# A 16-expert layer on one core: gate and up weights by four neighbouring rows per partition, token rows in that column order, the last four experts' rows finished apart

## The chip, the core and the metric

The kernel runs on one core of a Trainium2 chip. The metric is the device time of one execution in microseconds (us); the median of three runs is given, and one further execution was profiled. TensorE is called PE, VectorE DVE, ScalarE ACT, GpSimd POOL, SyncE SP, as in the profile.

## The reference, cut to what matters

512 tokens of width 1024 (16 learned tokens stand ahead of them) pass through one layer: an input LayerNorm, a two-branch mixer with an output projection, a LayerNorm, a mixture of 16 experts, and a last LayerNorm.

```python
h = layer_norm(concat(meta, x), ln_in_g, ln_in_b)
proj = h @ w_in                                   # (528, 9248)
mixed = (gate0 * ssd(proj) @ w_ssd_out + gate1 * pool(proj)) @ w_out
h = layer_norm(2 ** 0.25 * h + mixed, ln1_g, ln1_b)
# router: softmax over 16 experts; the best of 4 groups of 4; the best 2 in it
for e in range(16):
    a = silu(h @ w_gate[e]) * (h @ w_up[e])       # 1024 x 512 each
    out += comb[:, e:e+1] * (a @ w_down[e])       # 512 x 1024
h = layer_norm(2 ** 0.25 * h + out, ln2_g, ln2_b)
return h[:, 16:]
```

All is float32. Each token uses two experts of one group.

## The kernel before

**Head.** The tokens lie in four tiles `xt[t]` of 128 rows. POOL multiplies them by the gain and adds the bias of the input LayerNorm (L531, L532), and SP stores each tile to `h_dram` (L533), from where it is read back as `vt` some 600 us later. The buffers `xt` are then used again by the chain that makes the step sizes of the SSD branch (L538 to L572, on DVE and ACT).

**Mixer.** Until about 680 us PE multiplies by weights that are split into two parts (`wh`, `wl`), three matmuls for one. The output projection ends in `post` (L970): DVE adds the projection's PSUM tile to the tokens' rows in `vt`, half a row (512 columns) at a time. The router, and `place` (L1086), which brings the first two experts' tokens into column form by matmuls against a selection matrix, follow.

**Experts.** `order` lists the experts: the first of each of the four groups, then the second ones, and so on, so that the last four entries are the fourth experts of the four groups, and any four entries in a row from one such round have no token in common. Up to 96 tokens of an expert are gathered from DRAM by `gather` (L264, POOL), transposed in `xprep` (L1113), multiplied in `gu` (L1101, and `gu_third` for tokens beyond 64) and `down` (L1299), and added to `o_dram` by `add_rows` (L1350, two accumulating scatters on POOL). `fetch` (L1239) loads the weights on SP's queue, two loads of 1 MB for each of gate, up and down, into 22 buffers of 1 MB that are handed out in turn by `slot` (L1234).

PE contracts over 128 rows of a weight at a time. Which 128 rows is free as long as the tokens' columns are taken in the same choice. `rows2` puts two neighbouring rows of gate or up in a partition, in runs of 4 KB, and `cols2` takes the tokens' columns in steps of two:

```python
E.dma_start(r.rearrange("p (q j) c -> p q (j c)", j=2),
            src[r0:r0 + n, :].rearrange("(q p j) c -> p q (j c)", p=128, j=2))
...
c0 = k // 2 * 256 + k % 2
return v[:, c0:c0 + 255:2]
```

The rows after the second LayerNorm's gain and bias go to `o_dram` (L1203 to L1208) ahead of the expert loop: DVE writes four tiles of 128x1024, POOL issues their four stores.

**Tail.** The last two experts stand outside the loop (L1519 to L1615), where `InOrder` (L81) keeps DVE, ACT and POOL in the order of the text. Four tiles of `o_dram` are loaded when the add of the fourth expert from the end has landed (`order[12]`, 0-based: experts 13, 14 and 15 are then missing). The class `Finish` (L1409) makes the last LayerNorm of rows: `stats` and `scales` (DVE), or `sums` (ACT), `root` and `steps`; `scaled` (ACT), `gain` (DVE) and `store` (POOL, an accumulating scatter into the output, which holds the last bias already). Tokens of the last three experts are left out of the tiles' stores by the index `rest` and are gathered and finished apart: those of experts 13 and 14 in two tiles `hb`, those of 15 together with its down-projection `pye`, which is kept in PSUM.

Elsewhere the framework's scheduler, which estimates every instruction's time, orders the instructions of each engine.

Of the kernel before, what the change touches and what calls it, by code (L numbers as in the profile page):

```python
# [92 lines left out]
def hybrid_kernel(ctx, tc, x, meta_tokens, ln_in_g, ln_in_b, w_router, w_in, conv_w, conv_b,  # L93
# [60 lines left out]
    for q in range(4):  # L154
# [17 lines left out]
    C_G, C_B, C_CB, C_PS, C_BG, C_NW, C_DT, C_AL, C_DS, C_G1, C_B1 = (  # L172
        0, 8, 16, 48, 56, 72, 88, 89, 96, 112, 120)
# [51 lines left out]
    def rows2(E, r, src, r0):  # L225

        n = r.shape[1] * 128
        E.dma_start(r.rearrange("p (q j) c -> p q (j c)", j=2),
                    src[r0:r0 + n, :].rearrange("(q p j) c -> p q (j c)", p=128, j=2))

    def cols2(v, k):

        c0 = k // 2 * 256 + k % 2
        return v[:, c0:c0 + 255:2]
# [25 lines left out]

    def lim(v):
        return dict(bounds_check=v.shape[0] - 1, oob_is_err=False)

    def gather(dst, src, ix):  # L264
        n = ix.shape[0]
        return G.indirect_dma_start(out=dst[:n], out_offset=None, in_=src, in_offset=off(ix), **lim(src))


    with ExitStack() as p1:
# [120 lines left out]
        xm = hd.tile([NM, D], F32, name="xm")  # L390
# [19 lines left out]
        rows(ln1_g, C_G1, 8)  # L410
        rows(ln1_b, C_B1, 8)
# [241 lines left out]
        Q.dma_start(wr[:, 0], w_router.rearrange("(k p) e -> p k e", p=128))  # L653
        for t in range(NT):
            Q.dma_start(out[t * 128:(t + 1) * 128, :], bcast_row(ln2_b, D))
        for i, v in enumerate((ln1_g, ln1_b)):
            Q.dma_start(gb1[:, i, :].rearrange("p (q j) -> p q j", j=2),
                        flat(v).rearrange("(q p j) -> p q j", p=128, j=2))
        V.tensor_mul(wrg, wr[:, 0], cols[:, C_G1:C_G1 + 8, None].to_broadcast([128, KT, NE]))
        V.tensor_mul(wr[:, 1], wr[:, 0], cols[:, C_B1:C_B1 + 8, None].to_broadcast([128, KT, NE]))  # L660
# [280 lines left out]
        with tc.high_priority():  # L941
# [3 lines left out]
            rows2(G_, first, wu[order[0]], 512)  # L945
# [15 lines left out]
        for r, src, r0 in ((wg_[1], wg[order[0]], 512), (wg_[0], wg[order[0]], 0), (wu_[0], wu[order[0]], 0)):  # L961
            rows2(Q, r, src, r0)
# [15 lines left out]
        def router(t):  # L978
# [107 lines left out]
        def place(t):  # L1086
# [5 lines left out]
            for k in range(KT):  # L1092
                T.matmul(xps[k // 4][:, k % 4, :CAP], lhsT=cols2(vt[t], k), rhs=R0s[t][:, :CAP],
# [589 lines left out]
```

## Time and profile before

| what | us |
|---|---|
| median of 3 runs (lowest, highest) | 1038.21 (1037.29, 1038.98) |
| the profiled execution, its own time | 1038.58 |
| its span in the trace | 1036.8 |
| PE busy in the span | 946.0 |
| DVE, ACT, POOL busy | 594.0, 350.5, 167.5 |
[...]

The 2 us between span and time lie outside what the trace shows. The profile is read by stages: 0 to 680 us is the head and the mixer, 680 to 740 the post-projection, router and first expert, 740 to 975 the expert loop with all weights streaming, 975 to 1024 the last experts and the last LayerNorm; after that the last stores land and the program ends.

### The profile page before, as it was taken

To read this page: it belongs to the slowest core of one execution; us is meant where nothing else is said; L and a number is where in the kernel's file an instruction comes from. 1 tells how busy PE (TensorE), PEld (TensorE's weight loads), DVE (VectorE), ACT (ScalarE), POOL (GpSimd) and SP (SyncE) were. 2 spreads that over 40 slices of the span, in tenths; PEclk is the share of its full clock that TensorE was granted. 3 is DMA by queue.
4 is the path that set the end of the run, shared out by engine and by line. 5 is a ranking of instruction groups with operands and counts; after the bars stand their busy time and mean duration, and the time that the engine had idled before them with its cause. 6 is when DMAs were issued, how large, how long until landed. Compare 5 with 4: busy or idle time off the path is not lost. (4 is left out here: it accounts for less than half of the span.)

```text
span 1036.8 us, 19979 instructions
## 1 busy us (share of the span) xinstructions
PE 946.0 (91%) x8460; PEld 757.0 (73%) x8460; DVE 594.0 (57%) x1180; ACT 350.5 (34%) x503; POOL 167.5 (16%) x150
## 2 busy tenths in 40 slices
PE   4879999999999999999999897999779788999980
PEld 3878888999899898989898785877545344564550
DVE  6877671376869696978878778666520101001173
ACT  4344332532435252433425353224112121112252
POOL 4930000000000000000000226200212121212343
PEclk9999999999999999999999998999989899999996
DMA  7442446422323142333332423977899999999744
GB/s 220 138 162 100 131 131 178 122 82 82 134 90 128 56 151 74 123 102 123 102 122 72 153 91 133 379 290 304 293 367 372 373 373 374 371 372 373 251 123 78
DMA packets 98739, 199.43 MB, mean 192 GB/s; under 512 B 10272, under 2 KB 56968, under 8 KB 97616
## 3 DMA queue, kind: packets, MB, share of 16 engines
q1 hardware_dynamic: 83392, 163.78, 44.8%
q0 software_dynamic: 9392, 18.61, 7.2%
q10 hardware_dynamic: 5856, 15.61, 4.1%
q8 instruction: 76, 1.25, 0.5%
q14 instruction: 23, 0.19, 0.1%
HBM read 185.79 MB, written 19.79 MB: 198 GB/s over the span
## 5 line engine op out<-in xcount | busy, mean ns | idle before, releaser
L255 DVE TENSOR_TENSOR wl<-raw,wh 128x2048 fp32r<-128x2048 f32 (+1 forms) x49 | 111.7, 2283 | 53.2 <-ACT wh L252 53.0
L252 ACT CAST wh<-raw 128x2048 fp32r<-128x2048 f32 (+1 forms) x49 | 87.9, 1798 | 143.6 <-PE ss L800 64.1
L307 PE MATMUL mm<-hH,wh 128*128 128x264 f32 x624 | 128.7, 287 | 6.1 <-ACT ze L599 5.4
L89 PE MATMUL gu<-raw,xT 128*32 128x256 f32 (+1 forms) x2592 | 126.8, 344 | 7.8 <-issue 4.0
L307 PE MATMUL mm<-hH,wl 128*128 128x264 f32 x624 | 128.0, 286 | 0.0
L307 PE MATMUL mm<-hL,wh 128*128 128x264 f32 x624 | 127.3, 285 | 0.0
L89 PEld LDWEIGHTS gu<-raw,xT 128*32 128x32 f32 x2592 | 82.8, 110 | 48.8 <-issue 16.8
L1153 DVE TENSOR_TENSOR sg<-sg,gu 128x128 f32<-128x128 f32 x13 | 3.7, 288 | 182.5 <-ACT sg L1152 182.5
L307 PEld LDWEIGHTS mm<-hH,wh 128*128 128x128 f32 x624 | 99.1, 190 | 9.4 <-ACT ze L599 5.6
L809 POOL TENSOR_TENSOR acc<-acc,pre 128x512 f32<-128x512 f32 x12 | 19.1, 1614 | 530.5 <-ACT pre L808 530.5
L325 PE MATMUL mm<-hH,wh 128*128 128x512 f32 x256 | 102.5, 401 | 0.0
L325 PE MATMUL mm<-hL,wh 128*128 128x512 f32 x256 | 101.6, 397 | 0.0
L325 PE MATMUL mm<-hH,wl 128*128 128x512 f32 x256 | 101.5, 396 | 0.0
L307 PEld LDWEIGHTS mm<-hH,wl 128*128 128x128 f32 x624 | 98.0, 189 | 1.2 <-DVE wl L255 0.2
L307 PEld LDWEIGHTS mm<-hL,wh 128*128 128x128 f32 x624 | 97.4, 189 | 0.2
L89 PE MATMUL py<-raw,hT 128*32 128x512 f32 (+1 forms) x704 | 73.8, 558 | 5.2 <-issue 4.6
L800 PE MATMUL ss<-wh,yy 128*128 128x512 f32 x192 | 67.3, 410 | 0.0
L89 PEld LDWEIGHTS py<-raw,hT 128*32 128x32 f32 x704 | 23.5, 116 | 46.2 <-issue 39.2
L325 PEld LDWEIGHTS mm<-hH,wl 128*128 128x128 f32 x256 | 48.2, 188 | 10.5
L325 PEld LDWEIGHTS mm<-hH,wh 128*128 128x128 f32 x256 | 48.1, 188 | 10.3
L325 PEld LDWEIGHTS mm<-hL,wh 128*128 128x128 f32 x256 | 48.0, 188 | 10.3
L1256 POOL DMA_INDIRECT o_dram<-ys,ixq x26 | 40.5, 1557 | 74.3 <-ACT ys L1354 70.7
(391 smaller groups left out, 1584.1 us busy)
## 6 DMA issues: line engine op xcount, KB each, us to landing
raw<-in_w_exp_down_dram SPq DMA_DIRECT2D x30, 1024.0 KB
raw<-in_w_in_dram SPq DMA_DIRECT2D x28, 1024.0 KB
raw<-in_w_exp_up_dram SPq DMA_DIRECT2D x28, 1024.0 KB
raw<-in_w_exp_gate_dram SPq DMA_DIRECT2D x26, 1024.0 KB
M<-aD ACTq DMA_DIRECT2D x8, 1024.0 KB
raw<-in_w_in_dram SPq DMA_DIRECT2D x16, 512.0 KB
raw<-in_w_ssd_out_dram SPq DMA_DIRECT2D x8, 1024.0 KB
ze<-eD ACTq DMA_DIRECT2D x16, 256.0 KB
```

The lines of the kernel that those rows point to most:

```text
L89: return lambda *a, **k: self.tc.keep_in_program_order(f(*a, **k))
L252: A.copy(wh[:, c], src[:, c])
L255: (E[i] if E else V).tensor_sub(wl[:, c], src[:, c], wh[:, c])
L307: T.matmul(ps[:, i, :HF], lhsT=w[:, k, cs], rhs=h[k][:, i * HF:(i + 1) * HF], start=(n == 0), stop=(n == 3 * KT - 1))
L325: T.matmul(ps, lhsT=w[:, k, cs], rhs=h[k][:, NM:], start=(n == 0), stop=(n == 3 * KT - 1))
L800: T.matmul(ps, lhsT=y[:, j, t * 128:(t + 1) * 128], rhs=w[:, j, hf * 512:(hf + 1) * 512], start=(n == 0), stop=(n == 5))
L809: G.tensor_add(a, a, f)
L1153: V.tensor_mul(sg[:, 256:384], sg[:, 256:384], p3[:, 128:])
L1256: return G.indirect_dma_start(out=dst, out_offset=off(ix), in_=src[:n], in_offset=None, **lim(dst), **kw)
```

## The change

It has three parts. Gate and up weights go four neighbouring rows to a partition (one run of 8 KB for each partition and load, 512 rows a load), and the tokens' rows from the output projection on are kept in that column order: within each half row of 512, column 4r+j stands at 128j+r. `xprep`, `place` and the router then read neighbouring columns. Rows go into that order where POOL adds the first LayerNorm's bias (`by4`), where `post` reads PSUM, and back (`back4`) where the rows go to `o_dram`; since `xp` is a further buffer, each `h_dram` store leaves from the buffer that the tile before lay in. `o_dram` is written in half rows, by ACT's queue instead of POOL's. In the tail, four experts' rows instead of three stand apart, and the four tiles are loaded and finished one expert earlier; expert 13's rows get scales by themselves.

```diff
-    def rows2(E, r, src, r0):
+    def fours(E, r, src, r0):
+        E.dma_start(r.rearrange("p j c -> p (j c)"), src[r0:r0 + 512, :].rearrange("(p j) c -> p (j c)", j=4))
+    def by4(v):
+        return v.rearrange("p (r j) -> p j r", j=4)
+    def back4(v):
+        return v.rearrange("p (j r) -> p r j", j=4)
...
+        xp = hd.tile([128, D], F32, name="xp", tag="xm", bufs=1)
         for t in range(NT):
             G.tensor_mul(xt[t], xt[t], gb[:, 0, :])
-            G.tensor_add(xt[t], xt[t], gb[:, 1, :])
-            Q.dma_start(h_dram[t * 128:(t + 1) * 128, :], xt[t])
+            for c in (slice(0, 512), slice(512, 1024)):
+                G.tensor_add(xp[:, c].rearrange("p (j r) -> p j r", j=4), by4(xt[t][:, c]), by4(gb[:, 1, c]))
+            Q.dma_start(h_dram[t * 128:(t + 1) * 128, :], xp)
+            xp = xt[t]
...
-            V.scalar_tensor_tensor(vt[t][:, c], vt[t][:, c], ALPHA, pso, op0=OP.mult, op1=OP.add)
+            v = vt[t][:, c].rearrange("p (j r) -> p j r", j=4)
+            V.scalar_tensor_tensor(v, v, ALPHA, by4(pso), op0=OP.mult, op1=OP.add)
...
-                T.matmul(xps[k // 4][:, k % 4, :CAP], lhsT=cols2(vt[t], k), rhs=R0s[t][:, :CAP],
+                T.matmul(xps[k // 4][:, k % 4, :CAP], lhsT=vt[t][:, k * 128:(k + 1) * 128], rhs=R0s[t][:, :CAP],
...
-                    T.transpose(ps[i][:, k, :n], cols2(xg[:n], 4 * i + k), ident[:n, :n])
+                    T.transpose(ps[i][:, k, :n], xg[:n, (4 * i + k) * 128:(4 * i + k + 1) * 128], ident[:n, :n])
...
             for t in range(NT):
-                V_.tensor_mul(vt[t], vt[t], g1B)
-                V_.tensor_add(vt[t], vt[t], b1B)
-                G.dma_start(o_dram[t * 128:(t + 1) * 128, :], vt[t])
+                for c in (slice(0, 512), slice(512, 1024)):
+                    V_.tensor_mul(to.rearrange("p (r j) -> p r j", j=4), back4(vt[t][:, c]),
+                                  g1B[:, c].rearrange("p (r j) -> p r j", j=4))
+                    V_.tensor_add(to, to, b1B[:, c])
+                    A.dma_start(o_dram[t * 128:(t + 1) * 128, c], to)
+                    to = vt[t][:, c]
...
-                for e_ in order[-3:]:
+                for e_ in order[-4:]:
...
+    fin = Finish(fv[:NT] + rows4[:3], None)
+    add_to(down(i - 2, w2), i - 2)
+    rows_of(3, 1)
+    rows_of(0, 0)
+    for t in range(NT):
+        fin.stats(t)
+    fin.scales(slice(0, NT))
     pg = gu(wg2)
...
+    for t in range(NT):
+        fin.scaled(t)
+        fin.gain(t)
+    fin.store(0, rest[:, 0:1])
+    add_to(down(i - 1, w3), i - 1)
+    for t in range(1, NT):
+        fin.store(t, rest[:, t:t + 1])
...
     py = down_split(us, hhl)
-    fin.scaled(NT - 1)
-    fin.gain(NT - 1)
-    for t in range(2, NT):
-        fin.store(t, rest[:, t:t + 1])
-    fin.sums(NT)
-    fin.stats(NT + 1)
+    fin.sums(NT + 1)
+    fin.scales(slice(NT + 1, NT + 2))
+    fin.scaled(NT + 1)
+    fin.stats(NT + 2)
...
+    for n in (3, 2):
+        fin.gain(NT + n)
+        fin.store(NT + n, ix_of(last - 3 + n))
```

How the instructions move, at three places. SP's queue in the head: `raw<-in_w_in_dram` are the mixer's weights, `h_dram<-xt` the four stores. Before:

```order
L298 DMA raw<-in_w_in_dram 128x8x256 x2
L605 DMA raw<-in_w_pool_dram 128x2x256
L533 DMA h_dram<-xt 128x1024
L298 DMA raw<-in_w_in_dram 128x8x256
L533 DMA h_dram<-xt 128x1024 x3
```

Now:

```order
L310 DMA raw<-in_w_in_dram 128x8x256 x2
L618 DMA raw<-in_w_pool_dram 128x2x256
L310 DMA raw<-in_w_in_dram 128x8x256
L545 DMA h_dram<-xp 128x1024
L545 DMA h_dram<-xt 128x1024 x2
L310 DMA raw<-in_w_in_dram 128x8x256
L545 DMA h_dram<-xt 128x1024
```

All four stores stand behind a third weight load, and the last one behind a fourth.

POOL's queue in the tail (`o_dram<-ys` are the adds of an expert's rows, `raw<-o_dram,idx` and `hb<-o_dram,idx` the gathers of rows that stand apart, `out_dram<-raw,rest` the stores of the four tiles). Before, from the add of expert 13:

```order
L89 DMA o_dram<-ys_6570,ixq_113 1024x512
L89 DMA o_dram<-ys_6570,ixq_114 2048x256
L1307 UNCONDITIONAL_BRANCH
L89 DMA hb<-o_dram,idx 96x1024
L89 DMA o_dram<-ys_6569,ixq_113 1024x512
L89 DMA o_dram<-ys_6569,ixq_114 2048x256
L1134 UNCONDITIONAL_BRANCH
L89 DMA hb<-o_dram,idx 96x1024
L89 DMA out_dram<-raw,rest 512x1024 x4
L89 DMA out_dram<-hb,idx 512x1024 x2
L89 DMA out_dram<-raw,idx 512x1024
```

Now, from the store of the first tile:

```order
L89 DMA out_dram<-raw,rest 512x1024
L89 DMA o_dram<-ys_6589,ixq_113 1024x512
L89 DMA o_dram<-ys_6589,ixq_114 2048x256
L89 DMA out_dram<-raw,rest 512x1024 x3
L1327 UNCONDITIONAL_BRANCH
L89 DMA o_dram<-ys_6588,ixq_113 1024x512
L89 DMA o_dram<-ys_6588,ixq_114 2048x256
L89 DMA hb<-o_dram,idx 96x1024
L1148 UNCONDITIONAL_BRANCH
L89 DMA out_dram<-hb,idx 512x1024
L89 DMA raw<-o_dram,idx 96x1024
L89 DMA out_dram<-hb,idx 512x1024
```

The tiles' stores moved ahead of the last add (expert 14's); behind it stand four stores of single experts' rows, two more following the last line shown.

DVE's queue at the very end, from the last part of the split of expert 15's hidden rows (`raw<-pt,raw`). Before:

```order
L89 TENSOR_TENSOR raw<-pt,raw 128x4x32
L89 TENSOR_TENSOR raw<-raw 128x1024
L89 BN_STATS st<-hb 128x6 x2
L89 BN_AGGR mvf<-st 128x2
L89 SCALAR_TENSOR_TENSOR raw<-pye,wsl,raw 96x512
L89 BN_STATS st<-raw 128x6
L89 TENSOR_SCALAR rsf<-mvf 128x2
```

Now:

```order
L89 TENSOR_TENSOR raw<-pt,raw 128x4x32
L89 TENSOR_SCALAR rsf<-mvf 128x1
L89 TENSOR_SCALAR rsf<-rsf 128x1 x7
L89 SCALAR_TENSOR_TENSOR rsf<-mvf,rsf 128x1
L89 BN_STATS st<-raw 128x6 x2
L89 BN_AGGR mvf<-st 128x2
L89 SCALAR_TENSOR_TENSOR raw<-pye,wsl,raw 96x512
L89 BN_STATS st<-raw 128x6
L89 TENSOR_TENSOR hb<-hb,raw 128x1024
L89 SCALAR_TENSOR_TENSOR raw<-pye,wsl,raw 96x512
```

The fourth tile's gain is gone from here; the nine small instructions of expert 13's scales and the gain of its rows stand in the row now.

## Rows read from the trace of the kernel before

**Rows 1.** Windows: busy us (x count) of PE, PEld, DVE, ACT, POOL, clock, DMA share, GB/s.
```profile
733.00:975.00 242.00, 212.26 (x3400) 122.69 (x3396) 38.81 (x123) 47.15 (x122) 57.89 (x47) 0.94 1.02 370
```
**Rows 2.** Waits of PE, 733 to 975 us: total us, times, longest.
```profile
PE pt L89 <- DMA xg<-h_dram,idx: 9.3, 1, 9.3
```
**Rows 3.** DMA queues, 733 to 975 us: packets, MB, share of 16 engines.
```profile
q1 hardware_dynamic: 20720, 79.86, 86.3%
q0 software_dynamic: 5600, 8.95, 14.8%
...
raw<-in_w_exp_up_dram SPq DMA_DIRECT2D x22, 1024.0 KB
```
**Rows 4.** DMA, 888 to 892 us: only weight packets of 4 KB move.
```profile
DMA packets 423, 1.63 MB, mean 408 GB/s; under 512 B 25, under 2 KB 25, under 8 KB 423
```
**Rows 5.** DMA, 315.54 to 317.14 and 370.96 to 372.56 us: only 8 KB packets move.
```profile
DMA packets 84, 0.69 MB, mean 430 GB/s; under 512 B 0, under 2 KB 0, under 8 KB 0
DMA packets 81, 0.66 MB, mean 415 GB/s; under 512 B 0, under 2 KB 0, under 8 KB 0
```
**Rows 6.** Timeline and groups of PE's weight loads: every second column; neighbouring; `place`.
```profile
968.82 1.04 PEld L89 LDWEIGHTS pt<-ident,xg 96*128 96x128 f32 x8 [0.27 <-issue]
977.51 0.31 PEld L89 LDWEIGHTS pt<-ident,sg 128*128 128x128 f32 x3 [0.41 <-issue]
L89 PEld LDWEIGHTS pso<-xg,v 128*128 128x128 f32 x64 | 7.8, 196 | 1.2 <-ACT to L1067 0.6 <-DVE xg L1053 0.6
```
**Rows 7.** Groups of DVE: `post`; a reduction that reads apart; a product of neighbours.
```profile
L972 DVE SCALAR_TENSOR_TENSOR v<-v,pso 128x512 f32<-128x512 f32 x7 | 4.7, 676 | 4.9 <-PE pso L89 4.9
L663 DVE TENSOR_REDUCE raw<-wrg 128x16 f32<-128x128 f32 x1 | 0.4, 371 | 0.0
L659 DVE TENSOR_TENSOR wrg<-raw,cols 128x128 f32<-128x128 f32 x1 | 0.3, 293 | 1.8 <-DMA raw<-in_w_router_dram 1.8
```
**Rows 8.** Groups of POOL: the head's adds, the `o_dram` stores.
```profile
L532 POOL TENSOR_TENSOR xt<-xt,gb 128x1024 f32<-128x1024 f32 x4 | 12.9, 3258 | 0.0
L1208 POOL DMA_DIRECT2D o_dram<-v x4 | 2.2, 554 | 8.4 <-DVE v L89 8.4
```
**Rows 9.** Timeline, 60 to 72 us: start, us, engine, line, operation, idle before.
```profile
60.36 2.10 SPq L533 DMA_DIRECT2D h_dram<-xt  x3
67.75 0.43 DVE L543 TENSOR_SCALAR xt<-xt 128x528 f32<-128x528 f32 x1 [2.96 <-DMA h_dram<-xt]
70.98 0.81 PE L307 MATMUL mm<-hH,wh 128*128 128x264 f32 x2 [5.40 <-ACT ze L599]
```
**Rows 10.** Timeline of the tail, 981 to 1025 us.
```profile
981.28 2.41 SPq L1530 DMA_DIRECT2D raw<-o_dram  x4
981.79 0.62 DVE L89 TENSOR_TENSOR sg<-sg,gu 128x256 f32<-128x256 f32 x2 [10.49 <-PEq L1134]
987.90 1.64 PEld L89 LDWEIGHTS gu<-hb,xT 128*32 128x32 f32 x32
1007.32 5.80 PE L89 MATMUL pye<-raw 128*96 128x512 f32 x24 [1.60 <-ACT raw L89]
1008.69 1.23 ACT L89 ACTIVATE raw<-raw,rsf 128x1024 f32<-128x1024 f32 x1
1009.83 1.04 ACT L89 ACTIVATE raw<-hb 128x1024 f32<-128x1024 f32 x1
1011.10 1.28 DVE L89 BATCH_NORM_STATS2 st<-hb 128x6 f32<-128x512 f32 x2
1019.91 1.23 DVE L89 TENSOR_TENSOR raw<-raw 128x1024 f32<-128x1024 f32 x1 [0.22 <-ACTq L1623]
1019.97 2.48 POOL L89 DMA_INDIRECT out_dram<-hb,idx  x1 [0.59 <-DVE hb L89]
1022.75 1.43 POOL L89 DMA_INDIRECT out_dram<-raw,idx  x1 [0.30 <-issue]
```
**Rows 11.** DMA, 1012 to 1016 us: the accumulating stores' queue.
```profile
q0 software_dynamic: 259, 0.61, 101.3%
```

More of the change, by code (lines that the diff above doesn't have):

```diff
@@ L258, in off, with queued @@
         return bass.IndirectOffsetOnAxis(ap=ix, axis=0)
+    queue = []
+    def queued(f):
+        if not queue:
+            return f()
+        with tc.issue_after(queue[-1]):
+            r = f()
+        queue.append(r.ins)
+        return r
     def lim(v):
@@ L944, in hybrid_kernel @@
                 G_.dma_start(vt[t], h_dram[t * 128:(t + 1) * 128, :])
-            rows2(G_, first, wu[order[0]], 512)
+            fours(G_, first, wu[order[0]], 512)
             G_.dma_start(g1B, bcast_row(ln1_g, D))
@@ L1530, in hybrid_kernel, with rows_of, add_to @@
         last_['SP'] = Q.dma_start(fv[t], o_dram[t * 128:(t + 1) * 128, :]).ins
-    rows3 = fv[NT:NT + 3]
-    for v in rows3:
+    rows4 = fv[NT:]
+    for v in rows4:
         G.memset(v, 0.0)
-    gather(XG[(i + 1) % 2], h1_dram[:, :], ix_of(i + 1))
+    queue.append(gather(XG[last % 2], h1_dram[:, :], ix_of(last)).ins)
+    i = last - 1
+    V, A, G = (InOrder(tc, e_) for e_ in (V, A, G))
+    def rows_of(k, n):
+        ins = gather(rows4[k], o_dram[:, :], ix_of(last - 3 + k)).ins
+        if n:
+            apart(ins, n)
+        gets.append(ins)
+    def add_to(p, k):
+        for sc in add_rows(p, k):
+            for g_ in gets:
+                tc.declare_no_dep(sc, g_, reason="experts of different groups have no token in common")
+    gets = []
+    fin = Finish(fv[:NT] + rows4[:3], None)
[5 more added lines that the diff above has]
+    fin.scales(slice(0, NT))
     pg = gu(wg2)
@@ L1548, in hybrid_kernel, with part @@
     on = spare[1]
-    V.memset(fl(on)[CAP:], 0.0)
-    for w, (wh, wl) in zip(wd_, us):
-        A.copy(wh, w)
-        V.tensor_sub(wl, w, wh)
-    add_rows(down(i - 1, w3), i - 1)
-    def rows_of(k, ins, n):
-        ins.append(gather(rows3[k], o_dram[:, :], ix_of(last - 2 + k)).ins)
-        return ins[-1]
-    gets = []
-    apart(rows_of(2, gets, 2), 2)
-    rows_of(0, gets, 0)
-    fin = Finish(fv[:NT] + rows3[:2] + [fl(on)], fl(spare[0]))
-    tiles = slice(0, NT)
-    for t in range(NT):
-        fin.stats(t)
-    fin.scales(tiles)
+    fin.rows.append(fl(on))
+    fin.junk = fl(spare[0])
+    for t in range(NT):
[5 more added lines that the diff above has]
+        fin.store(t, rest[:, t:t + 1])
+    V.memset(fl(on)[CAP:], 0.0)
+    def part(k):
+        A.copy(us[k][0], wd_[k])
+        V.tensor_sub(us[k][1], wd_[k], us[k][0])
+    part(0)
+    fin.stats(NT)
+    fin.scales(slice(NT, NT + 1))
     pg = gu(wg_)
@@ L1571, in hybrid_kernel @@
     sg = silu(pg)
-    for sc in add_rows(down(i, wp_), i):
-        for g_ in gets:
-            tc.declare_no_dep(sc, g_, reason="experts of different groups have no token in common")
-    for t in range(NT - 1):
-        fin.scaled(t)
-        fin.gain(t)
-    for t in range(2):
-        fin.store(t, rest[:, t:t + 1])
-    rows_of(1, gets, 0)
+    part(1)
+    add_to(down(i, wp_), i)
+    rows_of(1, 1)
+    fin.scaled(NT)
+    fin.gain(NT)
+    fin.store(NT, ix_of(last - 3))
+    rows_of(2, 0)
     act(None, gu(wu_), p3=gu_third(last, (wg_, wu_)), sg=sg)
```

76 lines of the change are left out of this document (32 added, 44 removed).

## The prediction

> **What bounds the kernel now.** I read the busy times by stage first, because the change touches three stages with different limits. Until 733 us PE is the bound and the change does not alter its work there. From 733 to 975 us the DMA engines are: their share is 1.02, while PE is idle for 242 - 212.26 = 29.7 us [rows 1]. The reader is to see the two columns together, the full DMA share beside a PE that waits. The largest of these waits, 9.3 us for the third expert's gathered rows [rows 2], stands at the start of the stretch and costs nothing, since the weights arrive no faster for it; the other 20.4 us are shared out over the experts, mostly as waits for weights. The queues' view says what fills the DMA: 79.86 of 89.42 MB are weights on queue q1 [rows 3]. In the last two experts PE is the bound again, up to the last matmul, 1007.32 + 5.80 = 1013.1 us [rows 10]. Behind that stands a chain on DVE, ACT and POOL to the end of the last issue, 22.75 + 1.43 = 1024.2 us [rows 10], and the accumulating stores fill their queue for a part of it [rows 11]. Then the last store lands and the program ends, 12.6 us later; I leave this piece as it is.
>
> So a gain must come from the rate of the weights, from PE's last two experts or from the closing chain, and a loss from the head's order or from that chain.
>
> **The change, part by part.** The profiled execution took 1038.58 us, 0.37 above the median of the runs; sums go against the former, and the forecast is brought to the median at the end.
>
> *A. Runs of 8 KB.* The trace has both sizes. Where 4 KB weight packets move alone, the rate is 408 GB/s [rows 4], so a load of 1.049 MB takes 2.57 us. Where 8 KB packets move alone, it is 430 and 415 GB/s [rows 5], on average 422, and a load would take 2.49 us. By queue the same: 86.3% of 242 us on 16 engines over 20,720 packets is 161 ns for one of 4 KB [rows 3], so 256 of them take 2.58 us on 16 engines. 48 gate and up loads are issued from 733 us on, 24 of each (22 of the 24 up loads are the row in [rows 3]). 48 x 0.085 = **-4.1 us**. It counts in full, since it is taken from the stretch that the DMA bounds, and what PE has left to wait (20.4 us) is more than that. Bounds: nothing, if the mixed traffic has another limit; 48 x (2.57 - 2.44) = -6.3 at the better of the two rates. [...]
>
> *B. Neighbouring columns for PE.* In `xprep` 8 weight loads that read every second column take 1.04 us, 0.130 each; 3 that read neighbours take 0.31, 0.103 each [rows 6]. That is 0.2 us for an expert, of which the two experts that PE bounds count (0.4), and 16 x 0.027 = 0.4 for the last tile's `place`, whose loads are of the slow kind (196 ns) [rows 6]. I take **-0.7**; bounds -0.8 and 0.
>
> *C. `post` reads PSUM 16 bytes apart.* Now 676 ns for 512 columns [rows 7]. The nearest row that reads apart is a reduction over 128 columns, 371 ns, against 293 for a product of neighbours [rows 7]: at most 0.08 x 4 = 0.3 us. Seven of the eight lie beside PE's work, and only the last is waited for. **+0.2**, bounds 0 and +0.4.
>
> *D. `o_dram` in half rows on ACT's queue.* The four stores on POOL wait 8.4 us for DVE [rows 8], with the third expert's gather behind them; that gather now goes first and PE's 9.3 us wait becomes shorter, but the weights cover it. 1024 packets of 2 KB replace 512 of 4 KB in the stretch that the DMA bounds. A line through 161 ns at 4 KB and 311 ns at 8 KB (2.49 us x 16 / 128) gives 86 ns at 2 KB: (1024 x 86 - 512 x 161) / 16 = +0.35 us. ACT's eight issues wait for DVE, and behind them stand `xT` and `hT` of the first experts, where the DMA covers a delay. **+0.3**, bounds 0 and +1.
>
> *E. Head.* Four adds of 3258 ns on POOL [rows 8] become eight of half the size whose reads are 16 bytes apart; no row shows POOL reading so, and DVE's row bounds it at 371/293, 1.27 times, +3.4 us for the four. Then the stores: they are issued at 60.36 us, DVE waits 2.96 us for one of them to free its buffer, and PE waits 5.40 us soon after, for ACT [rows 9]. Each buffer is now freed by a later store, and the last store stands behind one more weight load that waits for its own buffer. What follows on DVE is the step-size chain and the next split of weights, which has about 5 us in hand. I take **+0.7**; bounds -0.5 (the issue order brings a weight load forward) and +5.
>
> *F. Tail.* The four tiles are loaded one expert earlier, so the issue at 981.28 us [rows 10] comes forward; their statistics stand on DVE ahead of expert 14's work, and DVE was idle for 10.49 us there [rows 10]. If the loads land about 5 us after the last weights, and 3.7 us of statistics and scales and 1.9 of `sg` and `xT` follow, PE's next need at 987.90 [rows 10] still has 2 us in hand. At the end: ACT no longer scales the fourth tile (1.23 us), so the sums of expert 13's rows begin at 1008.7 instead of 1009.83 [rows 10] and, at 2.64 us for the three large and small steps, end at 1011.3. Then DVE's new row: nine small instructions (2.2 us, as the nine of the four tiles' scales took), statistics of expert 14 (1.28 + 0.2), to 1015.0 where they began at 1011.10 before [rows 10]; first half product and its statistics 1.4, gain 1.2, second half 1.6 (by the 0.68 of `post` [rows 7] for a product, as much for its statistics), `root` and `steps` 1.3, to 1020.5; a scaling of 1.24 and then two gains, the second behind the second scaling, to 1024.2 where the last gain ended at 1019.91 + 1.23 = 1021.1 [rows 10]. The last issue would end at 1025.9 instead of 1024.2, since POOL's slow issue of 2.48 us [rows 10] loses its cause when the four tiles' stores have gone ahead. **+1.8**; bounds -2.5 (chain covered, that second of POOL and a shorter queue at the end) and +3.
>
> Sum: -4.1 - 0.7 + 0.2 + 0.3 + 0.7 + 1.8 = **-1.8 us**, 1036.8 for the profiled execution and **1036.4** for the median.
>
> **The rivals.** *1. The end is set by the stores' queue, not by the chain.* The queue of accumulating stores is full from 1012 to 1016 us [rows 11], and 2 MB of the four tiles pass it ahead of the last rows. Moved forward by a whole expert, they free it, and the last landing follows its issue at once. With F = -0.7 (what the queue gives back, 2.5, against the 1.8) and E = 0 the sum is -4.3: 1033.9. For it: the full queue and the slow issue of 2.48 us. Against it: the queue has gaps from 1018 us on, before the last issue.
>
> *2. The head stalls, and the kernel is slower.* POOL's strided adds and the last `h_dram` store behind a waiting weight load keep a buffer of the step-size chain; DVE, in order, sits before it, and the split of the next weights (2.3 us) comes late for PE. It decides once the store is more than about 5 us later. At twice that, PE loses about 6 in place of 0.7: +3.5, 1041.7. For it: DVE waited for such a store already [rows 9]. Against it: the 1.27 times from DVE's row give only 3.4 us. [...]
>
> *3. The longer runs bring nothing.* The two 8 KB stretches last 1.6 us each and carry nothing else, while the loop mixes weights with gathers and adds (q0: 14.8% of the time for a tenth of the bytes [rows 3]). If that mixture sets the rate, A is 0 and the sum is +2.3: 1040.5. For it: the mean over the whole stretch is 370 GB/s [rows 1], well below either rate. Against it: the weights' packets alone account for 86.3%.
>
> **How the numbers follow.** A difference under 0.2%, 2.1 us, can't be told from none. My forecast has a chance of 0.45 with a range of 1034.5 to 1038.5; its centre lies near the border, so 0.19 of it is faster and 0.26 the same. Rival 1 has 0.23, all faster. Rival 2 has 0.16, slower. Rival 3 has 0.10, of which 0.06 slower and 0.04 the same. 0.06 is left for parts that cancel, the same. Faster 0.42, same 0.36, slower 0.22. The range goes from 1031.3 (A at its better rate in rival 1, -2.2, and some of B's and C's play) to 1042.5 (rival 2 and D's bound).
>
> **What would show it.** In the changed profile: 733 to 975 us shorter by about 4 us, with 128 packets a gate or up load and about 311 ns a packet (A); weight loads of `xprep` near 0.10 us each (B); `post` under 1 us (C); PE's wait for the third expert's rows gone with no effect on the end (D); PE's first large wait still near 5 us and no new one of more than 2 us before 100 us (E); from the last matmul's end to the end of the last issue 13 us instead of 11 (F). I am wrong if the loop's stretch keeps its length, if PE shows a new wait in the head, or if statistics of the tiles hold `xT` of the last expert.

## The result and the profile after

The changed kernel is slower, where the forecast was 1036.4 us and its range ended at 1042.5.

| what | before | after |
|---|---|---|
| median, us (runs) | 1038.60 (4) | 1052.86 (4) |
| lowest, highest | 1037.29, 1040.06 | 1049.70, 1055.52 |
| ratio, with its 95% interval | | 1.0136 [1.0116, 1.0156] |
| the profiled execution, its own time | 1038.58 | 1049.70 |
| its span | 1036.8 | 1048.0 |
| its mean granted TensorE clock, share of full speed | 0.969 | 0.965 |

The profiled execution after is the fastest of its four, so the trace shows 11.1 of the 14.3 us. To place them I cut both spans at three instructions: SP's issue of the loop's first `down` load (731.17 us before, 732.14 after), the start of the loop's last transposes on PE, of the rows of expert 14 counted from 0 (968.82 [rows 6], now 971.00), and the end of the last issue (1024.18 [rows 10], now 1034.16 + 1.42 = 1035.58).

| stretch | before | after | difference | forecast |
|---|---|---|---|---|
| head and mixer | 731.17 | 732.14 | +1.0 | +0.7 (E) |
| expert loop | 237.65 | 238.86 | +1.2 | -4.3 (A to D) |
| tail, to the last issue | 55.36 | 64.58 | +9.2 | +1.8 (F) |
| to the end of the span | 12.62 | 12.42 | -0.2 | 0 |

**The loop.** The first row is the windows view of 733 to 975 us (columns as in [rows 1]), the second PE's largest wait there, the third SP's wait for a store, the fourth the weights' queue in the same stretch, the fifth the DMA view of 840 to 844 us, where weights move almost alone; the last two are from the kernel before, 733 to 975 us: SP's wait for a store, and the only waits of PE for weight loads in its list.

```profile
733.00:975.00 242.00, 208.33 (x3415) 118.04 (x3405) 42.38 (x131) 46.00 (x120) 56.58 (x43) 0.94 1.01 370
...
PE pt L89 <- DMA xg<-h_dram,idx: 9.8, 1, 9.8
...
SPq L1266 <- DMA o_dram<-v: 12.5, 3, 9.2
...
q1 hardware_dynamic: 14625, 80.07, 85.6%
...
DMA packets 246, 1.66 MB, mean 414 GB/s; under 512 B 40, under 2 KB 40, under 8 KB 48
...
SPq L1246 <- DMA o_dram<-v: 5.8, 2, 5.2
...
PE gu L89 <- DMA raw<-in_w_exp_down_dram: 1.0, 3, 0.3
```

The mean rate is 370 GB/s as before, at the same clock (0.94) [rows 1]: nearly a third of the packets are gone, and the bytes move no faster. PE's wait for the third expert's rows was to become shorter and is 9.8 us instead of 9.3 [rows 2]. SP waits for a store of `o_dram`, up to 9.2 us at once (5.2 before). Almost alone, 8 KB packets run at 414 GB/s, where 4 KB ones had 408 [rows 4].

Why the gather is not earlier stands on POOL's timeline (start, us, engine, line, operation, idle before it and what ended that):

```profile
747.96 0.95 POOL L1273 MEMSET xg<- 128x1024 f32 x1 [11.19 <-DMA o_dram<-room]
749.18 1.65 POOL L278 DMA_INDIRECT xg<-h_dram,idx  x1 [0.27 <-POOL xg L1273]
```

The stores left POOL's queue, as meant. But the first half row goes through a scratch buffer `room`, and the buffer of the third expert's rows is laid over it: POOL's memset waits 11.19 us for that store to land, and the gather is issued 17.04 us after the loop's first `down` load, where it was 16.77.

**Small loads, `post`, head.** PE's weight loads of `xprep` (the first row is that of the loop's last transposes) and `place` (the second row, a group); DVE's `post`; POOL's adds in the head and the last store of `h_dram`:

```profile
971.00 0.70 PEld L89 LDWEIGHTS pt<-ident,xg 96*128 96x128 f32 x8 [2.44 <-issue]
...
L89 PEld LDWEIGHTS pso<-xg,v 128*128 128x128 f32 x64 | 7.5, 192 | 1.2 <-ACT to L1081 0.6 <-DVE xg L1067 0.6
...
L986 DVE SCALAR_TENSOR_TENSOR v<-v,pso x7: 632/686/689, 682.5 to 710.1; 128x512 f32<-128x512 f32 x7
...
49.15 5.17 POOL L544 TENSOR_TENSOR xp<-xt,gb 128x512 f32<-128x512 f32 x2
54.28 18.55 POOL L544 TENSOR_TENSOR xt<-xt,gb 128x512 f32<-128x512 f32 x6
72.86 0.32 SPq L545 DMA_DIRECT2D h_dram<-xt  x1
```

Eight loads of neighbouring columns take 0.70 us (1.04 before [rows 6]); `place` has 192 ns for 196. `post` has a median of 686 ns before and after: here the reads of PSUM 16 bytes apart cost nothing. POOL's adds take 5.17 + 18.55 = 23.72 us instead of 12.9 [rows 8], 1.84 times, and the last `h_dram` store is issued at 72.86 us, where all four were out by 62.46 [rows 9]. That the adds are now halves is not the reason: POOL's twelve adds of 128x512 neighbouring columns later in the mixer (`acc<-acc,pre`) take 1620 ns on average, half of 3258.

**The tail.** First the DMA view (KB each, median us from issue to landing) of 945 to 970 us, then that of 970 to 991 us; then the timeline, whose last row is from the kernel before:

```profile
o_dram<-ys,ixq POOLq DMA_INDIRECT x3, 9.3
...
raw<-o_dram SPq DMA_DIRECT2D x4, 512.0 KB, 11.6
...
o_dram<-ys,ixq POOLq DMA_INDIRECT x2, 3.7
```

```profile
971.37 2.68 SPq L1551 DMA_DIRECT2D raw<-o_dram  x4
981.50 1.29 DVE L89 BATCH_NORM_STATS2 st<-raw 128x6 f32<-128x512 f32 x2 [8.35 <-DMA raw<-o_dram]
986.16 1.55 POOL L89 DMA_INDIRECT o_dram<-ys,ixq  x1 [15.80 <-ACT xT L89]
989.68 4.64 ACT L89 ACTIVATE raw<-raw,rsf 128x1024 f32<-128x1024 f32 x4 [3.97 <-DVE rsf L89]
996.94 0.47 ACT L89 COPY hT<-pt 128x384 f32<-128x384 f32 x1
997.47 5.34 PE L89 MATMUL py<-raw,hT 128*32 128x512 f32 x32 [3.69 <-ACT hT L89]
1009.28 1.54 POOL L89 DMA_INDIRECT o_dram<-ys,ixq  x1 [0.31 <-issue]
1012.77 5.79 PE L89 MATMUL pye<-raw 128*96 128x512 f32 x24 [1.60 <-ACT raw L89]
1017.05 1.06 ACT L89 ACTIVATE raw<-hb 128x1024 f32<-128x1024 f32 x1 [2.82 <-DMA hb<-o_dram,idx]
1030.20 2.36 DVE L89 TENSOR_TENSOR raw<-raw 128x1024 f32<-128x1024 f32 x2 [1.36 <-ACT raw L89]
1031.70 2.15 POOL L89 DMA_INDIRECT out_dram<-raw,idx  x1 [4.08 <-DVE raw L89]
1034.16 1.42 POOL L89 DMA_INDIRECT out_dram<-raw,idx  x1 [0.30 <-issue]
...
991.50 1.56 POOL L89 DMA_INDIRECT o_dram<-ys,ixq  x1 [12.29 <-DMA raw<-o_dram]
```

The four tiles are loaded one expert earlier, but that expert is still among the weights: the adds issued there take 9.3 us to land, and 3.7 later. So the loads are issued at 971.37, only 9.9 us before the old 981.28 [rows 10], and land 11.6 us after that (median of the four). Two queues then wait for them, and in both `InOrder` keeps the order of the text:

- ACT scales the tiles only when DVE has their scales, at 989.68. Behind the four scalings stand the copy `hT` of expert 14's hidden rows (996.94) and with it PE, which waits 3.69 us for it (0.62 before). The 32 matmuls behind that wait then take 5.34 us, where e5 below has 3.64 for the same ones: the granted clock from 990 to 1000 us is 0.89 (1.00 before). PE's last matmuls begin at 1012.77, 280.6 us after the loop's first `down` load (276.15 before).
- POOL's next add into `o_dram`, expert 12's rows, may not overwrite what is still being read, and goes at 986.16 (974.50 for its like before). The row names ACT as what ended 15.80 us of idleness, but `ys` had been done since 976.6; what ended it is the loads' landing, as the like row of e2 below names it. In the kernel before the first add behind the loads waited for them too, to 991.50, 10.2 us after their issue. Behind the add stand the tiles' stores, which wait for the scalings and gains: expert 14's add goes at 1009.28, the gather of expert 13's rows at 1012.98, their sums at 1017.05 where I had 1008.7.

From the last matmul's end to the end of the last issue it is 1035.58 - 1018.56 = 17.0 us, against 11.1 before and 13 in the forecast.

### The profile page after: what moved, and what is told of

The parts are those of the page before. It is cut to its first block, busy times and chain, and to the rows that moved or that the text cites. A ratio compares the mean times of both kernels' runs of the same rounds, so it can differ in the third digit from the quotient of the medians.

```text
span 1048.0 us, 20025 instructions
## 1 busy us (share of the span) xinstructions
PE 944.6 (90%) x8460; PEld 752.7 (72%) x8460; DVE 608.0 (58%) x1208; ACT 352.3 (34%) x504; POOL 184.5 (18%) x153
## 5 line engine op out<-in xcount | busy, mean ns | idle before, releaser
L822 POOL TENSOR_TENSOR acc<-acc,pre 128x512 f32<-128x512 f32 x12 | 19.2, 1620 | 521.0 <-ACT pre L821 521.0
L89 PE MATMUL py<-raw,hT 128*32 128x512 f32 (+1 forms) x704 | 75.9, 567 | 10.4 <-issue 6.7
L1276 POOL DMA_INDIRECT o_dram<-ys,ixq x24 | 37.3, 1553 | 69.2 <-ACT ys L1374 65.6
```

What stands on the lines that cost most here:

```text
L89: return lambda *a, **k: self.tc.keep_in_program_order(f(*a, **k))
L822: G.tensor_add(a, a, f)
L1276: return queued(lambda: G.indirect_dma_start(out=dst, out_offset=off(ix), in_=src[:n], in_offset=None, **lim(dst), **kw))
```

## The experiments

Ratios are against the kernel before, with 95% intervals.

### Which part: the two halves apart

*e1*: the change with the tail of before. *e2*: the kernel before with the tail of the change.

```diff
-                for e_ in order[-4:]:
+                for e_ in order[-3:]:
...
-    queue.append(gather(XG[last % 2], h1_dram[:, :], ix_of(last)).ins)
+    gather(XG[(i + 1) % 2], h1_dram[:, :], ix_of(i + 1))
```

> The changed kernel with the closing part of the kernel before (last three experts' rows apart, tiles loaded behind expert 12's add); runs of 8 KB and the new column order stay. Theory 1, the new tail lost the time: 1039 to 1042 us, and the last matmul ends within 3 us of the kernel before. Theory 2, the head and the expert loop lost it and the tail only inherits: 1048 us or more.

> The kernel before with the new closing part alone (last four experts' rows apart); weights in runs of 4 KB and the old column order. Theory 1: 1047 to 1051 us, with the add of expert 12 waiting about 10 us for the tiles' loads. Theory 2: within 3 us of the kernel before.

Measured: e1 1.0051 [1.0027, 1.0074], e2 1.0143 [1.0116, 1.0171]. Both halves lose. e1 should have won 3.6 us by terms A to E and loses 5; in its profile none of that lies in the loop (237.4 us against 237.65), 4.3 us lie ahead of the loop's first `down` load and 2.4 in the tail. The tail alone loses 14.9 where F had 1.8. In e2 the chain is that of the change: the add of expert 12 waits for the loads, and PE for `hT`.

```profile
985.78 1.55 POOL L89 DMA_INDIRECT o_dram<-ys,ixq  x1 [17.46 <-DMA raw<-o_dram]
...
997.28 6.60 PE L89 MATMUL py<-raw,hT 128*32 128x512 f32 x32 [4.53 <-ACT hT L89]
```

The two do not add up: 0.51 + 1.43 is more than the 1.36 per cent of both together. What the two halves share, or which of the runs' scatter makes up the rest, I did not find.

### The tail: what stands behind the waits

*e5*: the change, with the tiles' scaling, gain and stores moved behind expert 14's add and both gathers. *e5b*: the same in e2.

```diff
-    for t in range(NT):
-        fin.scaled(t)
-        fin.gain(t)
-    fin.store(0, rest[:, 0:1])
     add_to(down(i - 1, w3), i - 1)
-    for t in range(1, NT):
-        fin.store(t, rest[:, t:t + 1])
...
     rows_of(1, 1)
+    rows_of(2, 0)
+    for t in range(NT):
+        fin.scaled(t)
+        fin.gain(t)
+        fin.store(t, rest[:, t:t + 1])
     fin.scaled(NT)
     fin.gain(NT)
     fin.store(NT, ix_of(last - 3))
-    rows_of(2, 0)
```

> The changed kernel, with the four tiles' scaling, gain and stores moved behind the add of expert 14 and behind both gathers of the rows of 13 and 14, on ACT, DVE and POOL; the tiles' loads and statistics stay as early as in the change. If the loss of the tail is the place of this work in ACT's and POOL's order (PE waits 3.7 us for hT behind it; expert 13's rows are gathered at 1013 us behind the tiles' stores): PE's wait goes, the last matmul ends about 3 us earlier, the sums of expert 13's rows begin at least 4 us earlier, and the time falls by 4 to 8 us. If the loss is that add 12 waits for the tiles' loads: add 12 still starts near 986 us and the time stays within 2 us of the changed kernel.

> The same order of the tail as e5_late_tiles, on the kernel before with 4 KB runs (e2_new_tail with that one edit). By the first theory 4 to 8 us under e2_new_tail; a time under the kernel before would make four experts' rows apart worth having without the rest of the change.

Measured: e5 1.0105 [1.0068, 1.0142] against the change's 1.0136, e5b 1.0065 [1.0046, 1.0084] against e2's 1.0143. Between e5 and the change the intervals overlap; between e5b and e2 they do not. The trace of e5:

```profile
988.05 1.55 POOL L89 DMA_INDIRECT o_dram<-ys,ixq  x1 [16.25 <-ACT xT L89]
...
997.25 3.64 PE L89 MATMUL py<-raw,hT 128*32 128x512 f32 x32 [0.62 <-ACT hT L89]
...
1012.65 7.93 PE L89 MATMUL pye<-raw 128*96 128x512 f32 x24 [1.60 <-ACT raw L89]
...
1014.02 1.04 ACT L89 ACTIVATE raw<-hb 128x1024 f32<-128x1024 f32 x1
```

PE's wait for `hT` is back at 0.62 us, as before the change, and its last matmuls begin at 277.7 instead of 280.6 (both from the loop's first `down` load). The sums of expert 13's rows begin 1.4 us after that (4.3 in the change), although the add of expert 12 waits as long as in the change (16.25 us): what made them late is the tiles' work ahead of them, not that wait. From the end of the last matmul to the end of the last issue it is 12.0 us, and 13 was forecast, but that meets by luck: the last matmuls take 7.93 us here (5.79 in the change), and the granted clock from 1000 to 1024 us is 0.86 (0.93 in the change). From their start it is 19.9 us, where the forecast comes to 18.6. In e5b PE has other waits in their place:

```profile
993.69 3.07 PE L89 MATMUL gu<-raw,xT 128*32 128x256 f32 x32 [2.82 <-DVE xT L89]
```

Here it is the tiles' statistics on DVE that hold the last expert's columns, one of the three signs by which the prediction said that it would be wrong; in the change and in e5 PE does not wait there.

*e6*: the change, with the tiles' loads issued by POOL, so that SP's queue can't be what delays them.

```diff
...
-        last_['SP'] = Q.dma_start(fv[t], o_dram[t * 128:(t + 1) * 128, :]).ins
+        G.dma_start(fv[t], o_dram[t * 128:(t + 1) * 128, :])
```

> The changed kernel with the four tiles' loads issued by POOL instead of SP, so that they don't stand behind 14 us of weights on SP's queue. If that queue makes add 12 wait: it starts at 978 to 981 us instead of 986.2, and the time falls by 3 to 6 us. If the transfers as such are too slow beside the weights, add 12 starts within 2 us of 986 and the time stays.

Measured: 1.0136 [1.0095, 1.0177], the change's own ratio.

```profile
974.77 2.26 POOL L1551 DMA_DIRECT2D raw<-o_dram  x4 [1.27 <-DMA o_dram<-ys,ixq]
...
990.08 1.65 POOL L89 DMA_INDIRECT o_dram<-ys,ixq  x1 [13.05 <-ACT xT L89]
```

The loads still wait for expert 11's add to land, and expert 12's add goes as late behind them (254.1 us after the loop's first `down` load, 254.0 in the change); SP's queue is not the cause.

### The loop: length of the runs

*e3*: the kernel before with one run of 8 KB a partition. *e7*: with runs of 2 KB. Both leave out the matching order of the tokens' columns (as does e9 below): they do the same work on other pairs of numbers. The diff is e3's.

```diff
-        E.dma_start(r.rearrange("p (q j) c -> p q (j c)", j=2),
-                    src[r0:r0 + n, :].rearrange("(q p j) c -> p q (j c)", p=128, j=2))
+        E.dma_start(r.rearrange("p j c -> p (j c)"), src[r0:r0 + 512, :].rearrange("(p j) c -> p (j c)", j=4))
```

> The kernel before, with gate and up loads in runs of 8 KB and nothing else; the tokens' columns stay as they were, so the experts' matmuls pair other columns with other rows. If a load of 8 KB runs is faster by the 0.085 us that I forecast: 1034 to 1035 us. If by a third of that: about 1037. If not at all: 1038 to 1039, and the loop's stretch keeps its mean rate of 370 GB/s.

> The kernel before with gate and up loads in runs of 2 KB (one row for each partition and part); the tokens' columns stay as they were, so the experts' matmuls pair other columns with other rows. Theory: a small transfer waits behind the packets of the weights' queue, the longer they are the longer (the third expert's gather lands 9.0 us after its issue at 4 KB, 11.9 at 8 KB). Then at 2 KB it lands in less than 8 us and SP's longest wait for the o_dram stores is under 5.2 us, and the time is 1034 to 1039 us, as far as the shorter packets' own cost allows. Rival: the longer runs stream worse by themselves; then the latency of the gather is 9 us as before and the time within 2 us of the kernel before.

Measured: e3 1.0048 [1.0032, 1.0065], e7 1.0035 [1.0017, 1.0053]. 8 KB runs alone lose 5 us. The waits of PE and SP in e3's loop, and the windows view of 753 to 773 and 773 to 793 us:

```profile
PE pt L89 <- DMA xg<-h_dram,idx: 12.1, 1, 12.1
...
SPq L1244 <- DMA o_dram<-v: 8.7, 2, 8.3
```

```profile
753.00:773.00 20.00, 14.11 (x175) 6.80 (x179) 4.75 (x35) 3.33 (x8) 4.17 (x3) 0.74 0.97 335
773.00:793.00 20.00, 19.69 (x370) 12.10 (x358) 1.85 (x6) 3.77 (x10) 4.13 (x3) 1.00 0.91 333
```

PE waits 12.1 us for the third expert's rows, 9.3 before [rows 2], and 8.0 with 2 KB runs. SP waits 8.3 us for a store of `o_dram` to free the buffer of a weight load (5.2 before, none listed with 2 KB), and the DMA share falls to 0.91. The stores and the gather are small transfers of another queue beside the weights. In these three profiles, with runs of 2, 4 and 8 KB, the gather reaches PE 8.0, 9.0 and 11.9 us after its issue, and SP's longest wait for a store is 5.2 us with 4 KB and 8.3 with 8 KB. Why 2 KB runs end up slower too is open. The profiled execution of e7 is its longest, 1046.94 us where the median is 1042.27, and in it the loss is not in the loop: the last matmuls begin 274.2 us after the loop's first `down` load (276.15 before). Behind them DVE waits 5.84 us for a gather of rows, and the stretch up to that `down` load is 4.1 us longer, although its head is the old one.

### The loop: what stands ahead of the gather

*e4*: e1 with the eight half-row stores on POOL. *e10*: the kernel before with its four stores on ACT. *e9*: e3 with its four stores on ACT. The diff is that of e10 and e9.

```diff
-                G.dma_start(o_dram[t * 128:(t + 1) * 128, :], vt[t])
+                A.dma_start(o_dram[t * 128:(t + 1) * 128, :], vt[t])
```

> As e1_old_tail, but the eight stores of half rows to o_dram are issued by POOL instead of ACT. If ACT's queue makes the hole of the weight stream near 760 us (SP waits 9 us there for such a store), the hole goes and the time is 1 to 2 us under e1_old_tail. If the half rows themselves make it, the time is that of e1_old_tail within 1 us and SP still waits.

> The kernel before with the four stores to o_dram issued by ACT instead of POOL and nothing else. If the gather behind the stores costs the loop something at 4 KB too: the third expert's rows come at least 2 us sooner, the loop's last transpose starts 234 to 237 us after its first down load, and the time is 1 to 3 us under the kernel before. If the weights cover it, as I forecast: within 1 us of the kernel before.

> e3_runs_only (8 KB runs alone) with the four stores to o_dram issued by ACT instead of POOL, so that the third expert's gather goes ahead of them. In e3_runs_only the last transpose of the loop starts 243.5 us after the loop's first down load, in the kernel before 237.7, in the changed kernel 238.9. If the small transfers behind long packets made e3_runs_only slow, and the change gave that back by taking the gather out from behind the stores: 238 to 240 here, and 3 to 5 us under e3_runs_only. If the long runs cost it throughout the loop: 242 or more, and the time of e3_runs_only.

Measured: e4 1.0081 [1.0053, 1.0109], e10 **0.9956** [0.9939, 0.9973], e9 0.9970 [0.9950, 0.9991]. e10 beats both kernels, by 4.6 us over the one before (median 1034.10), and e4 shows the other direction: with eight issues ahead of it the gather goes at 20.9 us instead of e1's 16.8, and the kernel is, if anything, slower than e1. ACT and POOL in e10, PE's wait, and the windows view of 753 to 773 us in e10 and (last row) before:

```profile
740.63 11.03 ACTq L1208 DMA_DIRECT2D o_dram<-v  x4
...
743.25 1.71 POOL L266 DMA_INDIRECT xg<-h_dram,idx  x1 [0.27 <-POOL xg L1253]
...
PE pt L89 <- DMA xg<-h_dram,idx: 1.9, 1, 1.9
...
753.00:773.00 20.00, 18.64 (x340) 11.28 (x343) 6.22 (x41) 4.44 (x13) 4.61 (x4) 0.98 1.03 386
753.00:773.00 20.00, 16.06 (x239) 8.61 (x243) 4.76 (x35) 3.32 (x8) 4.17 (x3) 0.82 1.04 364
```

The gather is issued 10.18 us after the loop's first `down` load instead of 16.77, and PE's wait of 9.3 us becomes 1.9. The clock changes with it: from 753 to 773 us PE is granted 0.98 of its full clock in e10, and 0.82 before, 0.77 in the change and 0.74 in e3, where it comes out of waits of 9.3 to 12.1 us. How much of the 4.6 us is the wait and how much the clock these runs don't separate. And between e9 and e10, without the stores ahead of the gather, 8 KB runs no longer lose anything that stands out of the noise, and gain nothing: the 4.1 us of term A lie outside what the two sets of ten runs allow.

*e11*: e1 with the half rows' products in PSUM instead of in `room`. *e12*: the same in a buffer of another pool (its diff; e11 has `tp = ss()`).

```diff
-            to = room[:, 512:]
+            tp = psC.tile([128, 512], F32, name="pso")
...
-                    A.dma_start(o_dram[t * 128:(t + 1) * 128, c], to)
-                    to = vt[t][:, c]
+                    A.dma_start(o_dram[t * 128:(t + 1) * 128, c], vt[t][:, c])
```

> e1_old_tail with the products of the half rows kept in PSUM, so that no buffer of stores lies where the next gather's rows go (in the changed kernel POOL's memset of that buffer waits 11.2 us for the store of room to land, and the third expert's gather is issued 17.0 us after the loop's first down load; in e10_stores_act_4k 10.2). If that wait kept the change from the gain that e9_stores_act_8k and e10_stores_act_4k show: gather at 9 to 12 us, first transposes of the loop at 18 to 21 us instead of 25.8, the loop's last transpose 233 to 235.5 us after the first down load, and the time 2 to 5 us under e1_old_tail (near 1040). If the half rows on ACT's queue are slow by themselves: the last transpose stays at 237 us or later and the time is that of e1_old_tail.

> e11_no_scratch with the scratch in another PSUM bank, so that the memset that PE waits for stays ahead of the half rows on DVE. If the wait for the store of room kept the change from the gain: the first transposes of the loop start 18 to 21 us after its first down load (25.8 in e1_old_tail), the last ones 233 to 235.5 us (237.4), and the time is 2 to 5 us under e1_old_tail's 1.0051 of the kernel before, near 1.001. If not: the last transposes at 236.5 us or later and 1.004 or more.

Measured: e11 1.0040 [1.0013, 1.0066], e12 1.0024 [1.0002, 1.0046], e1 1.0051. The first rows are PE's waits in e11 and in e12, the third is the windows view of ten us in e12:

```profile
PE gu L89 <- DVE gu L1279: 7.3, 1, 7.3
```

```profile
PE pt L89 <- DMA xg<-h_dram,idx: 0.5, 1, 0.5
...
757.35:767.35 10.00, 9.58 (x120) 3.91 (x124) 5.28 (x37) 3.27 (x9) 3.10 (x2) 0.83 0.73 254
```

In e11 the products' PSUM buffer is shared with a tile that PE needs next, a wait in the place of the one removed. In e12 both waits are gone, but its time and e1's have overlapping intervals; the loop alone shows the gain. The runs that change the loop side by side, sorted by the start of the third expert's transposes on PE (us after the loop's first `down` load, and the start of the loop's last transposes):

| kernel | runs | gather issued | third expert | last transposes |
|---|---|---|---|---|
| e12 | 8 KB | 10.0 | 17.3 | 233.7 |
| e9 | 8 KB | 10.2 | 18.8 | 234.5 |
| e10 | 4 KB | 10.2 | 18.9 | 233.0 |
| e11 | 8 KB | 10.0 | 24.7 | 236.5 |
| e7 | 2 KB | 16.8 | 24.8 | 234.2 |
| before | 4 KB | 16.8 | 25.8 | 237.7 |
| e1 | 8 KB | 16.8 | 25.8 | 237.4 |
| after | 8 KB | 17.0 | 26.6 | 238.9 |
| e3 | 8 KB | 16.8 | 28.7 | 243.5 |
| e4 | 8 KB | 20.9 | 31.0 | 242.1 |

The end of the loop follows the start of the third expert, about 0.7 us for each: from 17.3 to 18.9 it lies at 233.0 to 234.5, from 28.7 on at 242.1 to 243.5. These are single profiles: the five other runs, which start the third expert at 25.9 to 26.4, end at 236.6 to 239.4. e7 and e3 lie 3.3 us below and above that line, so that a further effect of the runs' length is not excluded; between e9, e10 and e12 none shows. A gap in the stream does not show either: e12's row above is a stretch with a DMA share of 0.73 and 254 GB/s, and its loop is among the shortest.

### The head

*e8*: the kernel before with POOL's bias adds in eight halves that read and write 16 bytes apart, in place.

```diff
-            G.tensor_add(xt[t], xt[t], gb[:, 1, :])
+            for c in (slice(0, 512), slice(512, 1024)):
+                by4 = lambda v: v.rearrange("p (r j) -> p j r", j=4)
+                G.tensor_add(by4(xt[t][:, c]), by4(xt[t][:, c]), by4(gb[:, 1, c]))
```

> The kernel before, with the head's four bias adds on POOL cut into eight halves that read and write in steps of 16 bytes, in place (the rows keep their order). If the steps make POOL slow: the eight adds take 20 us or more against 12.9, and SP's first load of an expert's down weights after 725 us (the point from which I count the expert loop, 730 to 735 us in five profiles of the old head, 732 to 737 in five of the new) comes 2 to 3 us later than in most profiles of the old head; the time is 1040 to 1042 us. If the change's buffers and SP's order make the head slow instead: the adds stay long but the time stays within 1.5 us of the kernel before.

Measured: 1.0033 [1.0013, 1.0054], about +3.4 us. POOL's adds and PE's wait in e8, then the same wait in the change; then DVE's split of 128x2048 weights, in the change and twice before:

```profile
49.51 23.63 POOL L534 TENSOR_TENSOR xt<-xt,gb 128x512 f32<-128x512 f32 x8
...
PE mm L307 <- ACT ze L601: 6.7, 1, 6.7
...
PE mm L319 <- ACT ze L612: 3.8, 1, 3.8
```

```profile
66.64 4.21 DVE L256 TENSOR_TENSOR wl<-raw,wh 128x2048 fp32r<-128x2048 f32 x1
...
55.38 4.49 DVE L255 TENSOR_TENSOR wl<-raw,wh 128x2048 fp32r<-128x2048 f32 x1
...
69.31 2.28 DVE L255 TENSOR_TENSOR wl<-raw,wh 128x2048 fp32r<-128x2048 f32 x1
```

The adds take 23.63 us, as in the change, though they write 16 bytes apart as well. The wait of PE behind them grows from 5.40 [rows 9] to 6.7, but in the change it is 3.8: this wait is not where the change loses. What the traces show instead is a DVE that is slow while POOL works through these rows. The same split takes 4.49 us while POOL adds and 2.28 when it has finished, both in the kernel before; with the longer adds the one at 66.64 us still takes 4.21. Between 100 and 640 us PE is busy 530.9 us in each of five profiles with the old adds (before, e2, e3, e5b, e7), and 528.1 to 529.3 in six with strided ones (the change, e1, e4, e5, e6, e8): 1.6 to 2.7 us are lost there. In the change they are waits of PE for ACT's and DVE's parts of the next weights (`wh` 0.7, `wl` 0.6) and for `pm` (0.3), from 105 to 109 us, that the kernel before doesn't have. The time up to the loop's first `down` load is 732.8 us on average over the seven profiles with the old adds (730.1 to 735.3) and 735.2 over the seven with the whole new head (732.1 to 737.4), so that a single profile can't show it.

What e12 has left, 1.0024, is of the size of this one loss. Against e9, which has the same runs and the early gather without the new head, e12 is 0.54 per cent slower; whether the rest beyond e8's 0.33 is noise is open.

## Why the prediction was wrong

Forecast -1.8 us, measured +14.3. By its own terms:

**A, runs of 8 KB (-4.1): wrong; rival 3 had the outcome, by another mechanism than it named.** e9 against e10 gives 0.9970 to 0.9956, no gain. The step that failed took the packets' rate alone, from stretches of 1.6 us, and held that it counts in full "since it is taken from the stretch that the DMA bounds". Two things are wrong in it. The rate alone was too high: 414 against 408 GB/s is 1.5%, or 1.8 us on these 48 loads (1.049 MB each). And the DMA does not bound the stretch by its rate. I had read PE's 20.4 us of other idle time as "mostly as waits for weights"; in PE's list 1.0 us of it are waits for weight loads (the row stands above with the loop); most of the rest stands there under its own sequencer (9.9) and issue (8.6). SP issues a load when PE frees a buffer; in the loop of before it waits 57 times for PE, 158.2 of the 242 us in all, as in this group:

```profile
SPq L228 <- PE py L89: 31.9, 10, 8.9
```

So the DMA share of 1.02 there [rows 1] means that loads are always under way, not that PE would go on if they were faster.

**B (-0.7) and C (+0.2): too small to matter.** `xprep`'s eight loads gain 0.34 us an expert, more than the 0.2 I had; `place` gains 4 ns a load where I had 27, so its 0.4 did not come. `post` costs nothing.

**D, stores on ACT (+0.3): wrong by its cover.** I wrote that PE's 9.3 us wait becomes shorter "but the weights cover it". e10 takes only this wait away and wins 4.6 us [0.9939, 0.9973]: PE's lost time is not made up, and its clock is lower beside it (0.82 from 753 to 773 us, 0.98 in e10). In the change nothing was won, because the scratch buffer ties the gather to a store (11.19 us). I had followed the stores' move to another queue, not what shares memory with the new scratch.

**E, head (+0.7): inside its bounds, by another mechanism.** The failed step is POOL's strided add, bounded by DVE's row at 1.27 times; it is 1.84 times. The reading alone costs it: the change writes neighbours, e8 writes 16 bytes apart too, and both take the same time (23.72 and 23.63 us). That e8's +3.4 meets rival 2's +3.5 is luck. Rival 2 had DVE wait for a store that frees its buffer late; in the change DVE waits 0.77 and 1.21 us for such stores, 2.96 [rows 9] and 0.78 before, and is slow beside POOL instead (4.21 us for the split of 128x2048 at 66.64, 2.28 when POOL has finished).

**F, tail (+1.8): the largest miss.** The stretch is 9.2 us longer. 3.3 of them are PE's, from the loop's last transposes to the start of the last matmuls; 2.9 are the later start of expert 13's sums behind that; 1.3 are POOL's last issues; the remaining 1.7 are what I had for the chain. From the sums to the last gain that chain is right: 15.5 us forecast and 15.5 measured (1017.05 to 1030.20 + 2.36). Only its end is not: POOL's slow issue did not lose its cause when the tiles' stores had gone ahead, it takes 2.15 us (2.48 before [rows 10]), and the last issue ends 3.0 us after the last gain, as before, where I had 1.7.

What failed is the step before the chain. The loads were to land "about 5 us after the last weights"; an add that lands in 3.7 us after the weights takes 9.3 among them, so the loads came forward by 9.9 us only, and they then took 11.6 us from issue to landing. How long after the last weights that is no view here shows; but expert 12's add could go only 14.8 us after their issue, and in the kernel before the like add 10.2. PE's next need was met even so: at the place of the old 987.90 [rows 10] PE does not wait. But I had followed one engine, DVE, to that need, and not the queues behind it: ACT's `hT` behind the scalings (PE waits 3.1 us longer, and its next 32 matmuls take 5.34 us, 3.64 in e5), and POOL's add and gather behind the tiles' stores.

The ratio's other 3 us against the profiled run are the scatter of the change's four runs. Rival 1 (the stores' queue sets the end) did not come about: the last issue itself is late, and from there to the end of the span it is 12.4 us, 12.6 before, where the rival had 2.5 less. Its sum is also off by 0.7: with E = 0 and F = -0.7 the terms add up to -5.0, not -4.3.

**What stays open.** Why the halves' losses don't add up; why the 2 KB runs lose 3.7 us; what makes POOL's last issue but one slow; and whether a tail with four experts apart can win at all, when its loads are made to wait for nothing that is among the weights, was not tried.

## What to carry to other kernels

A load or a store that is moved forward goes into other company: take its time from issue to landing from the stretch that it moves into (9.3 us among the weights here, 3.7 behind them), and then follow every queue, those of a fixed order above all, behind each instruction that waits for it, beyond the first need that is met. Ask of an engine that gets longer work what it slows beside it: here DVE's split took 4.49 us beside POOL's adds and 2.28 behind them. The DMA share of 1.02 in this loop said that the queues were full, not that their rate set the time (e9 0.9970, e10 0.9956); look at what the issuing engine waits for, and whether a gap in the stream moves the end. And when a transfer is taken from one queue so that another can go first, look also at what shares memory with its buffers: one letter (the stores' queue, e10) gained 4.6 us where the same step with a scratch buffer gained nothing.

## What was not expected of the hardware

- POOL's adds of f32 with operands 16 bytes apart took 1.84 times as long (23.72 against 12.9 us for four tiles), while DVE read PSUM 16 bytes apart at no cost (686 ns, as before).
- While POOL worked through the head's rows, DVE's split of 128x2048 took 3.5 to 4.5 us; when it had finished, 2.28 (before and after).
- Behind the four stores on its own queue, the third expert's gather reached PE 8.0, 9.0 and 11.9 us after its issue with weights in runs of 2, 4 and 8 KB (e7, before, e3). With the stores on ACT's queue it was 8.7 and 8.6 us at 4 and 8 KB (e10, e9). In these single profiles the packets' length of the weights' queue told on the gather only where stores stood ahead of it.
- An accumulating scatter that lands in 3.7 us after the weights takes 9.3 us among them (medians of two and three; over the 24 of the whole stretch 9.4).
